# Adding feature tiles on VectorE ahead of the ones-matmuls of two layer norms, in a decoder layer on one core

## The chip, the core and the metric

The kernel runs on one core of a Trainium2 chip. The metric is device time in microseconds (us), the median of several runs. The profile is of one more execution.

## What is computed

One decoder layer on one sequence: x is 256 tokens by 2048 features, in float32. Everything a reader needs here is in the order of the stages and in the layer norm:

```python
mod = silu(c) @ w_ada + b_ada            # shift1, scale1, gate1, shift2, scale2, gate2
u = x*(1+scale1) + shift1
proj = u @ w_in                          # GLU input | q | k | v | two branch gates
hc = silu(layer_norm(causal_conv31(a_lin*sigmoid(a_gate)), conv_ln_g, conv_ln_b))
y_conv = hc @ w_conv_out + b_conv_out    # hc: 256 x 1024
y_attn = causal_attention(rope(q), rope(k), v) @ w_attn_out
mix = (g_conv*y_conv + g_attn*y_attn) @ w_out
x = layer_norm(ALPHA*x + (1+gate1)*mix, ln1_g, ln1_b)
u = x*(1+scale2) + shift2
x = layer_norm(ALPHA*x + (1+gate2)*conv_swiglu(u, w_up, w_down), ln2_g, ln2_b)

def layer_norm(x, g, b):
    mu = x.mean(-1); var = square(x - mu).mean(-1)
    return (x - mu) * rsqrt(var + 1e-5) * g + b
```

## The kernel before

Activations lie feature-major: a tile has 128 features on the partitions and the 256 tokens along the free axis. x is 16 such tiles, in `xT[0]` (0 to 7) and `xT[1]` (8 to 15); the convolution's output `cacc` is 8 tiles.

**Matmuls.** Weights stream through five `raw` buffers of 512 KB (`chunk`, from L380). Each chunk is split into two float32r parts, `wh` (a cast on ScalarE, L393) and `wl` (a subtraction on VectorE, L394), and each product is three matmuls: high by high, high by low, low by high (`feat`, L405 to L407). A `raw` buffer is free again once its `wl` is made.

**adaLN.** The modulation's weights `w_ada` go through the same five buffers, but not to TensorE: VectorE multiplies each chunk by a column of silu(c) and adds it to `acc` (L207). All loads of both kinds are issued by SP, in one queue. So an L207 or L394 that comes late on VectorE holds back the load that wants its buffer, and all loads behind it.

**Background work.** While weights are streamed, `chunk` advances generators: the adaLN pieces, the attention, and a background queue `bg_q` with the convolution, its norm (`conv_norm`, L538) and the first half of the first norm's sums (`ln1_tiles`, L733). Each yields an estimate of its cost; the rates set how much runs per chunk. That gives the program order. The order on each engine is then made by a planner, which simulates the timeline and takes, of the instructions that are ready, the earliest in program order (`schedule_with_timeline_sim=True`).

**The norms.** The mean over features is a sum over partitions and over tiles. It is made on TensorE by a float32 matmul with an all-ones 128 x 128 matrix, one for each tile, accumulated in PSUM; every partition then holds the sum.

- `conv_norm`: 8 ones-matmuls for the mean (L542). Then for each half of four tiles VectorE subtracts the mean (L551, 1024 columns at once), ScalarE squares (L552), and TensorE adds the four squares into `pv` (L554). A small root loads the table (L555). Then the variance (L557), the root (L558), the reciprocal (L560), the products with it (L566), the swish (L568) and the split into `chi` and `clo`, which are the moving operand of the `w_conv_out` matmuls.
- The first norm: `w_out` is streamed in three groups, of tiles 0 to 7, 8 to 11 and 12 to 15. After a group the residual is made (L759). After the first group a rough mean `m0` of two tiles (L764, L765) is subtracted from all tiles, to keep the numbers small: from `xT[1]` in two pieces (L767), from `xT[0]` tile by tile (L735, in `ln1_tiles`, in the background of the second group). `stats` (L725) squares a tile on ScalarE (L728) and adds the tile and its square into the two halves of one PSUM bank, `stat[0]` and `stat[1]` (L729, L730). Tiles 8 to 11 and 12 to 15 get `stats` after their groups. After tiles 8 to 11 the adaLN pieces are run up to the ninth (`ada_until(NB)`), in program order ahead of the third group's weights.
- After the last `stats` the norm is finished (L801 to L807) and the first tiles of `u2h` are made, with which the `w_up` matmuls begin.

Of the kernel before, what the change touches and what calls it, by code (L numbers as in the profile page):

```python
# [8 lines left out]
F32 = mybir.dt.float32  # L9
F32R = mybir.dt.float32r  # L10
AF = mybir.ActivationFunctionType
OP = mybir.AluOpType
# [21 lines left out]
def layer_kernel(ctx: ExitStack, tc: tile.TileContext, x, c, w_ada, b_ada, w_in, conv_dw_w, conv_dw_b,  # L34
# [44 lines left out]

# [1 line left out]
    ident = cst.tile([128, 128], F32, name="ident")  # L81
# [53 lines left out]

# [1 line left out]
    xT = wide(0, F32, "xT")  # L137
# [19 lines left out]

# [1 line left out]
    mod = cst.tile([128, 96], F32, name="mod")  # L159
# [218 lines left out]

# [1 line left out]
    def chunk(src, width, two=False):  # L380
# [61 lines left out]

# [1 line left out]
    lin = slot(6, [128, 8, 256], F32, "lin")  # L444
# [63 lines left out]

# [1 line left out]
    cacc, chi = [None], []  # L510
# [27 lines left out]
    def conv_norm():  # L538
# [10 lines left out]
        for t in range(0, CT, CN):  # L549
            ts = slice(t, t + CN)  # L550
            nc.vector.tensor_tensor(a[:, ts], a[:, ts], mean[:, None, :].to_broadcast([128, CN, 256]), OP.subtract)  # L551
            nc.scalar.activation(sq[:, ts], a[:, ts], AF.Square)  # L552
            for j in range(t, t + CN):
                nc.tensor.matmul(pv[:, :256], ones, sq[:, j], start=j == 0, stop=j == CT - 1)  # L554
        nc.scalar.activation(mean[:, 0:1], sq[:, 7, 0:1], AF.Sqrt)  # L555
# [16 lines left out]

# [1 line left out]
    rps = []  # L574
# [75 lines left out]

# [1 line left out]
    ra0 = 1.0  # L652
# [72 lines left out]
    def stats(t):  # L725
        d = xT[t // 8][:, t % 8]
        sq = wk.tile([128, 256], F32, tag="t", bufs=4, name="sq1")
        nc.scalar.activation(sq, d, AF.Square)  # L728
        nc.tensor.matmul(stat[0], ones, d, start=t == 0, stop=t == KT - 1, skip_group_check=True)  # L729
        nc.tensor.matmul(stat[1], ones, sq, start=False, stop=t == KT - 1, skip_group_check=True)  # L730
        return sq

    def ln1_tiles():  # L733
        for t in range(8):
            nc.vector.tensor_tensor(xT[0][:, t], xT[0][:, t], m0, OP.subtract)  # L735
            stats(t)
            yield 0.34

# [5 lines left out]
    for t0, t1 in zip(cuts, cuts[1:]):  # L744
# [16 lines left out]
        if t0 == 0:  # L761
            pm = pst("pm0")
            for t in range(2):
                nc.tensor.matmul(pm[:, :256], ones, xT[0][:, t], start=t == 0, stop=t == 1)  # L764
            nc.scalar.activation(m0, pm[:, :256], AF.Copy, scale=1.0 / 256)  # L765
            for h in range(2):
                nc.vector.tensor_tensor(xT[1][:, h * 4:h * 4 + 4], xT[1][:, h * 4:h * 4 + 4],  # L767
                                        m0[:, None, :].to_broadcast([128, 4, 256]), OP.subtract)
            pms = pst("pms")
            stat = [pms[:, :256], pms[:, 256:]]  # L770
            bg_q.append(ln1_tiles())
        else:
            for t in range(t0, t1):
                sq = stats(t)
        if t0 == 8:
            nc.scalar.activation(lc[:, 0:1], sq[:, 0:1], AF.Sqrt)
            ada_until(NB)
            drain(bg_q)

# [1 line left out]
    def norm(k, n, center):  # L781
# [38 lines left out]

# [1 line left out]
    NP = 7  # L822
# [49 lines left out]

# [1 line left out]
    lrows = [slot(i, [128, D], F32, n) for i, n in ((14, "l2g"), (15, "l2b"))]  # L874
# [107 lines left out]
```

## Time and profile before

| | |
|---|---|
| median of three runs | 1479.33 us (1477.72 to 1479.35) |
| span of the profiled execution | 1477.4 us |
| TensorE (PE) busy | 1417.7 us, 96% |
| VectorE (DVE) busy | 1108.8 us, 75% |
| ScalarE (ACT) busy | 796.9 us, 54% |
| HBM read | 353.10 MB, 240 GB/s over the span |

In the profile PE is TensorE, DVE VectorE, ACT ScalarE and SP the engine that issues loads. L12 is line 12 of the kernel. A tile's name is followed by its inputs: `wl<-wraw,wh` is `wl` made from `wraw` and `wh`. Times in a timeline count from the start of the span. A busy share of an engine is an average over stages; matmuls are pipelined, and their ends in the trace are modelled. "acc3a" is the fourth PSUM bank of a group, "acc" the adaLN sum.

### The profile page before, as it was taken

The numbers are of one execution on the slowest core, as the hardware profiler recorded it, in microseconds if no ns is written. First come the engines' busy times: TensorE is split into PE (matmuls) and PEld (weight loads), VectorE is DVE, ScalarE is ACT, GpSimd is POOL, SyncE is SP. The second block draws the span as 40 slices with busy tenths as digits, with TensorE's granted clock in tenths as the row PEclk, the third lists the DMA queues.
The fourth block names the chain that finished last, engine by engine and source line by source line (L and its number), as shares of the span: only waits on it lengthen the run. The fifth ranks groups of instructions, "written<-read, shape, count | busy, mean of one in ns | idle before, by whom it ended". The sixth has DMA issues, their size and how long they took to land.

```text
span 1477.4 us, 26835 instructions
## 1 busy us (share of the span) xinstructions
PE 1417.7 (96%) x10691; PEld 1364.2 (92%) x10691; DVE 1108.8 (75%) x1398; ACT 796.9 (54%) x1250; POOL 27.7 (2%) x57
## 2 busy tenths in 40 slices
PE   4899999999999989998999999999999999999996
PEld 4889999989999989997999999999999998888886
DVE  6788888998989879896877767988765545446456
ACT  3546436669987655345545576555444444343342
POOL 2000000210000000000000000000000000000000
PEclk9999999999999999999999999999999999999998
DMA  9999899886567657987799977778776676655662
GB/s 310 328 302 334 299 339 310 256 280 209 175 194 222 210 173 254 310 297 226 242 307 315 323 248 218 240 246 254 238 217 183 180 224 215 193 172 173 189 202 100
DMA packets 154990, 358.53 MB, mean 243 GB/s; under 512 B 12172, under 2 KB 26466, under 8 KB 154608
## 3 DMA queue, kind: packets, MB, share of 16 engines
q1 hardware_dynamic: 152704, 352.37, 74.0%
q0 software_dynamic: 1872, 4.33, 0.9%
q8 instruction: 83, 1.36, 0.4%
q14 instruction: 43, 0.35, 0.1%
q10 hardware_dynamic: 288, 0.12, 0.0%
HBM read 353.10 MB, written 2.10 MB: 240 GB/s over the span
## 4 chain that ended last, share of the span: by engine, by line
PE 75%; DMA 13%; DVE 8%; issue 2%; ACT 2%; SPq 0%; DVEq 0%; ACTq 0%
DMA araw<-in_w_ada_dram 9%; PE acc0a L405 5%; PE acc0a L407 5%; PE acc0a L406 5%; PE acc1a L405 5%; PE acc1a L407 5%; PE acc1a L406 5%; PE acc2a L406 3%; PE acc2a L407 3%; PE acc2a L405 3%; PE acc3a L405 3%; PE acc3a L406 3%; PE acc3a L407 3%; DVE wl L394 3%; DVE acc L207 2%
## 5 line engine op out<-in xcount | busy, mean ns | idle before, releaser
L393 ACT CAST wh<-wraw 128x1024 fp32r<-128x1024 f32 (+1 forms) x483 | 496.7, 1030 | 559.5 <-PE acc3a L416 132.7
L394 DVE TENSOR_TENSOR wl<-wraw,wh 128x1024 fp32r<-128x1024 f32 (+1 forms) x483 | 577.1, 1198 | 252.1 <-ACT wh L393 248.1
L207 DVE SCALAR_TENSOR_TENSOR acc<-araw,ccol,acc 128x1024 f32<-128x1024 f32 (+1 forms) x182 | 225.4, 1238 | 84.3 <-DMA araw<-in_w_ada_dram 82.6
L405 PE MATMUL acc0a<-u2h,wh 128*128 128x256 f32 x352 | 99.3, 282 | 4.8 <-ACT u2h L325 4.8
L407 PE MATMUL acc0a<-u2h,wl 128*128 128x256 f32 x352 | 100.3, 285 | 3.1 <-DVE wl L394 3.1
L405 PE MATMUL acc1a<-u2h,wh 128*128 128x256 f32 x352 | 99.4, 283 | 0.0
L406 PE MATMUL acc0a<-u2l,wh 128*128 128x256 f32 x352 | 99.4, 282 | 0.0
L406 PE MATMUL acc1a<-u2l,wh 128*128 128x256 f32 x352 | 99.2, 282 | 0.0
L407 PE MATMUL acc1a<-u2h,wl 128*128 128x256 f32 x352 | 99.2, 282 | 0.0
L533 ACT ACTIVATE pr<-hc,cw 128x256 f32<-128x256 f32 x200 | 88.8, 500 | 11.7 <-DVE cacc L535 11.3
L405 PE MATMUL acc0a<-uh,wh 128*128 128x256 f32 x256 | 74.9, 292 | 7.1 <-ACT uh L242 7.1
L407 PE MATMUL acc0a<-uh,wl 128*128 128x256 f32 x256 | 74.5, 291 | 3.2 <-DVE wl L394 3.2
L406 PE MATMUL acc0a<-ul,wh 128*128 128x256 f32 x256 | 73.4, 287 | 1.6 <-DVE ul L243 1.6
L405 PE MATMUL acc2a<-uh,wh 128*128 128x256 f32 x256 | 73.1, 286 | 0.5 <-ACT gb L487 0.5
L406 PE MATMUL acc2a<-ul,wh 128*128 128x256 f32 x256 | 73.4, 287 | 0.0
L405 PE MATMUL acc1a<-uh,wh 128*128 128x256 f32 x256 | 73.3, 286 | 0.0
L407 PE MATMUL acc1a<-uh,wl 128*128 128x256 f32 x256 | 73.2, 286 | 0.0
L407 PE MATMUL acc2a<-uh,wl 128*128 128x256 f32 x256 | 73.2, 286 | 0.0
L406 PE MATMUL acc1a<-ul,wh 128*128 128x256 f32 x256 | 73.2, 286 | 0.0
L405 PE MATMUL acc3a<-uh,wh 128*128 128x256 f32 x256 | 73.2, 286 | 0.0
L407 PE MATMUL acc3a<-uh,wl 128*128 128x256 f32 x256 | 73.0, 285 | 0.0
L406 PE MATMUL acc3a<-ul,wh 128*128 128x256 f32 x256 | 72.9, 285 | 0.0
(438 smaller groups left out, 4349.8 us busy)
## 6 DMA issues: line engine op xcount, KB each, us to landing
araw<-in_w_ada_dram SPq DMA_DIRECT2D x176, 512.0 KB, 5.1
wraw<-in_w_up_dram SPq DMA_DIRECT2D x176, 512.0 KB, 4.8
wraw<-in_w_in_dram SPq DMA_DIRECT2D x144, 512.0 KB, 4.9
wraw<-in_w_down_dram SPq DMA_DIRECT2D x55, 512.0 KB, 4.5
wraw<-in_w_down_dram SPq DMA_DIRECT2D x44, 384.0 KB, 3.7
wraw<-in_w_out_dram SPq DMA_DIRECT2D x32, 512.0 KB, 5.5
araw<-in_w_ada_dram SPq DMA_DIRECT2D x32, 256.0 KB, 5.7
wraw<-in_w_attn_out_dram SPq DMA_DIRECT2D x16, 512.0 KB, 4.5
```

Of the source, the lines that this page charges most:

```text
L207: op = nc.vector.scalar_tensor_tensor(acc, r, ccol[:, k:k + 1], acc, OP.mult, OP.add)
L393: nc.scalar.copy(wh, raw)
L394: nc.vector.tensor_tensor(wl, raw, wh.bitcast(F32), OP.subtract)
L405: nc.tensor.matmul(o, wh[:, cs], ah, start=first and i % 2 == 0, stop=False, skip_group_check=True)
L406: nc.tensor.matmul(o, wh[:, cs], al, start=False, stop=False, skip_group_check=True)
L407: nc.tensor.matmul(o, wl[:, cs], ah, start=False, stop=last, skip_group_check=True)
L533: nc.scalar.activation(pr[:, k % 2, i], src, AF.Copy, scale=w)
```

## The change

Tiles are added to each other on VectorE before the ones-matmul, so that fewer ones-matmuls are issued.

- `conv_norm`: the eight squares are added to four and then to two (one instruction of 1024 columns, one of 512), and two ones-matmuls take the place of eight. They now follow both squares.
- `ln1_tiles`: `xT[0]` is centred and squared in two pieces of four tiles. Then the eight tiles, and the eight squares, are each added to four and to two, into `sm`, with two ones-matmuls each. The squares lie in slot 6, the sums in slot 16.
- Tiles 8 to 11 (`ln1_four`): one square of 1024 columns, one add of 512 columns for the tiles and one for the squares, two ones-matmuls each. The background queue is now drained ahead of this, not behind `ada_until(NB)`.
- Tiles 12 to 15 stay as they are.

```diff
@@ conv_norm
             nc.scalar.activation(sq[:, ts], a[:, ts], AF.Square)
-            for j in range(t, t + CN):
-                nc.tensor.matmul(pv[:, :256], ones, sq[:, j], start=j == 0, stop=j == CT - 1)
+        for n in (4, 2):
+            nc.vector.tensor_tensor(sq[:, :n], sq[:, :n], sq[:, n:2 * n], OP.add)
+        for j in range(2):
+            nc.tensor.matmul(pv[:, :256], ones, sq[:, j], start=j == 0, stop=j == 1)
@@ first norm
-        nc.tensor.matmul(stat[0], ones, d, start=t == 0, stop=t == KT - 1, skip_group_check=True)
+        nc.tensor.matmul(stat[0], ones, d, start=False, stop=t == KT - 1, skip_group_check=True)
...
+    def halves(dst, src, n):
+        nc.vector.tensor_tensor(dst[:, :n], src[:, :n], src[:, n:2 * n], OP.add)
+
     def ln1_tiles():
-        for t in range(8):
-            nc.vector.tensor_tensor(xT[0][:, t], xT[0][:, t], m0, OP.subtract)
-            stats(t)
-            yield 0.34
+        sq, sm = slot(6, [128, 8, 256], F32, "sqw"), slot(16, [128, 8, 256], F32, "sm")
+        for h in (slice(0, 4), slice(4, 8)):
+            nc.vector.tensor_tensor(xT[0][:, h], xT[0][:, h], m0[:, None, :].to_broadcast([128, 4, 256]), OP.subtract)
+            nc.scalar.activation(sq[:, h], xT[0][:, h], AF.Square)
+            yield 0.6
+        for j, src in enumerate((xT[0], sq)):
+            s = sm[:, j * 4:j * 4 + 4]
+            halves(s, src, 4)
+            yield 0.5
+            halves(s, s, 2)
+            for i in range(2):
+                nc.tensor.matmul(stat[j], ones, s[:, i], start=j + i == 0, stop=False, skip_group_check=True)
+            yield 0.5
+
+    def ln1_four():
+        sq = slot(6, [128, 8, 256], F32, "sqf")
+        d = xT[1][:, 0:4]
+        nc.scalar.activation(sq[:, 0:4], d, AF.Square)
+        for j, src in enumerate((d, sq[:, 0:4])):
+            s = sq[:, 4 + j * 2:6 + j * 2]
+            halves(s, src, 2)
+            for i in range(2):
+                nc.tensor.matmul(stat[j], ones, s[:, i], start=False, stop=False, skip_group_check=True)
+        return sq[:, 0]
...
+        elif t0 == 8:
+            drain(bg_q)
+            sq = ln1_four()
+            nc.scalar.activation(lc[:, 0:1], sq[:, 0:1], AF.Sqrt)
+            ada_until(NB)
         else:
             for t in range(t0, t1):
-                sq = stats(t)
-        if t0 == 8:
-            nc.scalar.activation(lc[:, 0:1], sq[:, 0:1], AF.Sqrt)
-            ada_until(NB)
-            drain(bg_q)
+                stats(t)
```

## Rows read from the trace of the kernel before

**Rows 1.** The page's first part: busy us, share of the span, instructions.

```profile
PE 1417.7 (96%) x10691; PEld 1364.2 (92%) x10691; DVE 1108.8 (75%) x1398; ACT 796.9 (54%) x1250; POOL 27.7 (2%) x57
```

**Rows 2.** TensorE's waits, 505 to 620 and 620 to 720 us: total, times, longest.

```profile
PE acc0a L405 <- ACT chi L242: 5.3, 1, 5.3
...
PE acc0a L405 <- ACT wh L393: 2.0, 1, 2.0
```

**Rows 3.** Windows: length, busy PE, PEld, DVE, ACT, POOL (instructions), clock, DMA share, GB/s.

```profile
533.20:538.80 5.60, 5.54 (x25) 5.41 (x26) 4.47 (x8) 4.85 (x12) 0.00 (x0) 0.50 0.39 135
...
668.20:671.90 3.70, 3.64 (x18) 3.65 (x19) 2.73 (x4) 2.66 (x7) 0.00 (x0) 0.54 0.85 285
...
540.00:550.00 10.00, 10.00 (x86) 10.00 (x85) 5.75 (x5) 3.14 (x3) 0.00 (x0) 1.00 0.52 156
```

**Rows 4.** VectorE's timeline, 520 to 534 us: start, us, engine, line [idle before].

```profile
520.53 1.22 DVE L394 TENSOR_TENSOR wl<-wraw,wh 128x1024 fp32r<-128x1024 f32 x1
523.57 1.28 DVE L207 SCALAR_TENSOR_TENSOR acc<-araw,ccol,acc 128x1024 f32<-128x1024 f32 x1 [1.82 <-DMA araw<-in_w_ada_dram]
524.77 0.68 DVE L706 TENSOR_TENSOR gb<-acc0a,gb 128x512 f32<-128x512 f32 x1
525.37 1.22 DVE L394 TENSOR_TENSOR wl<-wraw,wh 128x1024 fp32r<-128x1024 f32 x1
...
527.10 0.42 DVE L557 TENSOR_SCALAR pr<-pv 128x256 f32<-128x256 f32 x1
...
530.24 1.22 DVE L394 TENSOR_TENSOR wl<-wraw,wh 128x1024 fp32r<-128x1024 f32 x1
531.36 2.56 DVE L566 TENSOR_TENSOR cacc<-cacc,pr 128x256 f32<-128x256 f32 x5
```

**Rows 5.** VectorE's timeline, 635 to 651 us, columns as in rows 4.

```profile
634.99 2.35 DVE L767 TENSOR_TENSOR xT<-xT,ln 128x1024 f32<-128x1024 f32 x2
637.26 2.10 DVE L735 TENSOR_TENSOR xT<-xT,ln 128x256 f32<-128x256 f32 x6
639.27 1.28 DVE L207 SCALAR_TENSOR_TENSOR acc<-araw,ccol,acc 128x1024 f32<-128x1024 f32 x1
...
641.13 3.49 DVE L394 TENSOR_TENSOR wl<-wraw,wh 128x1024 fp32r<-128x1024 f32 x3
...
649.59 1.28 DVE L207 SCALAR_TENSOR_TENSOR acc<-araw,ccol,acc 128x1024 f32<-128x1024 f32 x1 [2.04 <-DMA araw<-in_w_ada_dram]
```

**Rows 6.** Waits of SP's load queue, 634 to 641 us, columns as in rows 2.

```profile
SPq L190 <- DVE xT L735: 5.4, 1, 5.4
```

**Rows 7.** One window of 2 us, columns as in rows 3.

```profile
640.00:642.00 2.00, 1.48 (x8) 1.19 (x7) 2.00 (x4) 2.00 (x6) 0.00 (x0) 1.00 0.21 25
```

**Rows 8.** The chain that ended last, 637 to 672 us: start, us, what.

```profile
643.52 5.97 DMA araw<-in_w_ada_dram
...
661.84 5.25 DMA wraw<-in_w_out_dram
```

**Rows 9.** VectorE's timeline, 664 to 671 us, columns as in rows 4.

```profile
664.49 3.92 DVE L207 SCALAR_TENSOR_TENSOR acc<-araw,ccol,acc 128x1024 f32<-128x1024 f32 x3
668.32 2.50 DVE L394 TENSOR_TENSOR wl<-wraw,wh 128x1024 fp32r<-128x1024 f32 x2
```

**Rows 10.** The tile `ones`: records, duration ns min/median/max, first and last start.

```profile
L729 PE MATMUL pms<-xT,ones x32: 377/379/484, 639.1 to 696.6; 128*128 128x256 f32 x32
...
L554 PE MATMUL pv<-sq,ones x16: 377/379/379, 523.2 to 526.5; 128*128 128x256 f32 x16
```

**Rows 11.** TensorE's timeline, two successive ones-matmuls, columns as in rows 4.

```profile
642.51 0.59 PE L730 MATMUL pms<-sq,ones 128*128 128x256 f32 x2
642.94 0.59 PE L729 MATMUL pms<-xT,ones 128*128 128x256 f32 x2
```

**Rows 12.** ScalarE's timeline, the squares of the convolution's norm, columns as in rows 4.

```profile
519.67 2.04 ACT L552 ACTIVATE sq<-cacc 128x1024 f32<-128x1024 f32 x2
```

## The prediction

> **What bounds the kernel now.** The page's first part comes first: TensorE is busy for 96% of the span, VectorE for 75% [rows 1]. By that row alone every TensorE microsecond taken out would be a microsecond won. But both changed places stand next to a wait, so the next view is TensorE's waits around them [rows 2]: 5.3 us, ended by ScalarE's `chi` (the convolution branch's output), behind the convolution's norm; and 2.0 us, ended by the cast `wh`, behind the first norm's sums of tiles 8 to 11. After each of the two the windows show a granted clock of 0.50 and 0.54, nearly all at the 1.2 GHz level: 25 matmul records in 5.6 us and 18 in 3.7 us, where a full stretch at 2.4 GHz has 86 in 10 us [rows 3]. A stage that ends in such a wait is set by what ends the wait, not by TensorE's work ahead of it. So I read what ends each.
>
> Wait one (528.0 to 533.3 us). VectorE's timeline [rows 4]: a split ends at 521.75 us, the adaLN step L207 starts at 523.57 us after 1.82 us of waiting for its DMA, and from there VectorE works without a gap up to the `cacc` products at 531.36 us, which feed the swish and `chi`. The variance (L557, 527.10 us) is one link in that row, and two splits that only the next group needs stand in it too (525.37 and 530.24 us). So VectorE's own queue, not only TensorE's sums, makes `chi` late.
>
> Wait two (666.1 to 668.3 us). VectorE's timeline from 635 us [rows 5]: two centrings of 1024 columns, six of the eight one-tile centrings, an adaLN step, the other two, and three splits, back to back; only at 647.5 us does it come to a pause, of 2.04 us, for an adaLN DMA. Each weight buffer is freed by a split or an adaLN step, so that block keeps SP waiting for 5.4 us before it can issue a load [rows 6], and the DMA share falls to 0.21 between 640 and 642 us [rows 7]. From there the chain of waits goes by transfers and VectorE and leaves TensorE out: the adaLN load issued at 643.52 us, then the `w_out` load issued at 661.84 us and landed 5.25 us later, whose cast lets TensorE go on [rows 8]. VectorE is full at the end of it as well: three adaLN steps in a row from 664.49 us and then the first split of the next group, at 668.32 us [rows 9]. So of this stretch VectorE and the loads set the end, and TensorE has time to spare.
>
> **The change part by part.** What it removes: a ones-matmul is two records (16 for 8 matmuls at L554, 32 for 16 at L729, and as many at L730) [rows 10], and two successive ones start 0.43 us apart [rows 11]. The convolution's norm goes from 8 to 2 (6 fewer). The first norm's tiles 0 to 7 go from 16 to 4 (12 fewer), its tiles 8 to 11 from 8 to 4 (4 fewer), tiles 12 to 15 stay. 22 x 0.43 = 9.5 us of TensorE: 2.6 ahead of wait one, 5.2 + 1.7 ahead of wait two.
>
> What it adds is on VectorE. An add of 1024 columns costs what the centring of that size costs: two of them occupy 634.99 to 637.26, 1.14 us each [rows 5]. One of 512 columns costs 0.60 us, the spacing of the L706 at 524.77 us and the split behind it [rows 4]. Convolution's norm: 1.14 + 0.60 = 1.74 us. First norm, tiles 0 to 7: two such pairs, 3.48 us, less what the wide centring saves (eight at 2.01 / 6 = 0.335 us are 2.68; two at 1.14 are 2.28; 0.40 saved) = +3.1 us. Tiles 8 to 11: two adds of 512, +1.2 us. On ScalarE the squares become fewer and wider; it isn't late in either stretch, and I cost that at nothing. No DMA is added. The squares' new slots, 6 and 16, had their last readers in the attention and convolution output stages, so no wait comes from them.
>
> A rule of the Trainium skill speaks the other way. The chain [rows 8] goes through VectorE and loads where TensorE is 96% busy over the span. The Trainium skill, "Perfetto Trace Analysis", section "Identifying the Most-Contended Engine", says to find the engine with the highest occupancy and to optimize that one first (it warns that for TensorE busy time flatters); applied to [rows 1] it makes this change worth the whole 9.5 us, which is the first rival below.
>
> Convolution's norm, on the path. The two adds can start when ScalarE has done the squares, at 521.7 us [rows 12], just when VectorE has its 1.82 us pause [rows 4]. If the planner, which sets each engine's order by its own simulated times, puts them ahead of L207, they are free, and as fewer sums follow, L557 and the products may overtake the two splits in the row, at 1.14 us each (the size of a centring): 2.3 us earlier. If it puts them behind L207, the gapless row gets longer by 1.74 us. Bounds -2.3 and +1.7; neither order is visible in the trace of before, so I take the middle, -0.3. TensorE's 2.6 us are worth nothing of themselves here: it arrives earlier and waits longer.
>
> First norm, tiles 0 to 7. L207 of 639.27 frees the next load's buffer; the two wide centrings stand ahead of it at least (2.28 against 2.01). The adds of the d tiles (1.74 us) are early in program order and ready at once, so they should come before or among the three splits from 641.13 us, and hold the load of 643.52 us back by about 1.74 - 0.40 = 1.3 us. The adds of the squares (1.74 us) come next and fit into the 2.04 us pause before 649.59 [rows 5]. What the load's delay costs is passed on by transfers, which are without a gap from there. Bounds: -0.4 us (all adds in pauses, the centring's saving kept) and +3.1 us (none hidden); taken +1.3.
>
> First norm, tiles 8 to 11. The two adds of 512 want VectorE between the last residuals and the split of 668.32 us, where it has no pause [rows 9]. Bounds 0 (they take a pause that the later loads open) and +1.2; I take +1.2, as the row is full. The 1.7 us saved on TensorE lie in its wait. If that cover were gone they would be a gain of 1.7. A longer wait could also prolong the stretch at 1.2 GHz behind it; the present one costs 3.7 - 18 x 0.116 = 1.6 us [rows 3]. Bound 0 to +1; taken 0, since the clock is down there already.
>
> Sum: -0.3 + 1.3 + 1.2 = +2.2 us. The profiled span is 1477.4 us; the median of the three runs, 1479.33 us, lies 1.9 us above it, and I keep that distance: 1477.4 + 2.2 + 1.9 = 1481.5 us.
>
> **The rivals.** First, TensorE is the limit in spite of the waits: both waits move up with its work, and 9.5 us are won, 1477.4 + 1.9 - 9.5 = 1469.8 us. For it: 96%. Against it: the two waits are ended by other engines, and the removed work lies directly ahead of them.
>
> Second, the convolution's chain gets shorter and VectorE's adds in the first norm disappear in pauses: -2.3 - 0.4 + 0 gives 1476.6 us. For it: the 1.82 us pause at the right moment. Against it: the first norm's adds would have to wait for a pause while they are ready much earlier.
>
> Third, slower: VectorE becomes the bound outright. Its place is the gapless block from 635 us; the adds stand ahead of the steps that free the load buffers, the 5.4 us wait of SP grows by the whole 3.1 us, the adds of tiles 8 to 11 by 1.2 more, and in the convolution's norm they stand behind L207 (+1.7): +6.0, 1485.3 us. It decides from the point where more than the 2.04 us of the pause in adds precede the adaLN step now at 649.59; with one half of it, without the convolution's 1.7, it gives 1483.6.
>
> Fourth, the change doesn't do only what it says: the planner orders all instructions anew, and other stages move by some microseconds in either direction, with the forecast's sum on top.
>
> **How the numbers follow.** About 0.2% (3 us) is what a measurement of this kernel can tell from no change. Forecast 0.45 (it reaches from -1.5 to +3.8 us, about 0.08 of it beyond +3), first rival 0.06, second 0.17 (0.08 of it beyond -3, where TensorE's saved time adds to it), third 0.26, fourth 0.06 (0.02 each way and 0.02 between). Faster 0.06 + 0.08 + 0.02 = 0.16; slower 0.08 + 0.25 + 0.02 = 0.35 (0.01 of the third falls short of +3); same 0.49. The forecast's own range is 1477.8 to 1483.1. Faster and slower cases together hold about half, so the range of 8 in 10 takes in the third rival's sum and most of the second: 1475.0 to 1485.6; the first rival is left out.
>
> **What would show it.** In the profile after: TensorE's records of the sums fall from 80 to 36 (16 + 32 + 32 to 4 + 16 + 16), its busy time by up to 9.5 us less what longer modelled records hide, while the span does not. The wait for `chi` is as long as before or longer, and starts earlier. The wait behind tiles 8 to 11 grows from 2 us to some 9 or 10, and its end moves later by 1 to 4 us against the `chi` wait's end. SP's wait during the centring block is 5.4 us or more. The forecast is wrong if the second wait's end comes closer to the first one's (then TensorE or the freed `wh` buffers did set the loads), or if `chi` moves by more than 2 us, or if a stage that the change doesn't touch moves as much as these.

## The result, and the profile after

| | before | after |
|---|---|---|
| median, runs side by side | 1479.34 us | 1491.31 us |
| ratio | | 1.0076 (95%: 1.0052 to 1.0101) |
| the same pair once more | 1482.54 us | 1491.58 us, 1.0068 (1.0050 to 1.0087) |
| span of the profiled execution | 1477.4 us | 1493.2 us |

The change makes the kernel slower by 0.7 to 0.8%, 9 to 12 us. The prediction (1481.5 us, at most 1485.6) had the sign of its sum right and the size wrong.

Line numbers shift a little: the residual L759 is L784 in after, L706 is L708, the variance L557 is L559, the reciprocal L562, the products L568. The convolution's adds are L554 and its sums L556; the first norm's wide centrings are L741, its adds L736, its sums L750 and L761.

The page's first part of after, against [rows 1]:

```profile
PE 1415.7 (95%) x10647; PEld 1361.0 (91%) x10647; DVE 1115.8 (75%) x1400; ACT 795.7 (53%) x1241; POOL 27.7 (2%) x57
```

The 44 records of the 22 removed ones-matmuls are gone (10691 to 10647), yet TensorE's busy time falls by only 2.0 us and the span grows. So time went into waits. TensorE's waits of after at the two places of [rows 2] (520 to 545 us, 636 to 700 us; total, times, longest):

```profile
PE acc0a L405 <- ACT chi L242: 6.2, 1, 6.2
PE pv L556 <- DVE sq L554: 4.9, 1, 4.9
...
PE acc0a L405 <- ACT wh L393: 6.9, 1, 6.9
PE pms L761 <- DVE sqf L736: 3.5, 1, 3.5
PE acc0a L407 <- DVE wl L394: 2.6, 1, 2.6
```

In before the two waits were 5.3 and 2.0 us. Now two sums wait for adds, and behind each of them the old wait has grown as well. VectorE's timeline of after around the convolution's norm (start, us, engine, line [idle before]), to be held against [rows 4]:

```profile
525.05 1.28 DVE L207 SCALAR_TENSOR_TENSOR acc<-araw,ccol,acc 128x1024 f32<-128x1024 f32 x1 [1.33 <-DMA araw<-in_w_ada_dram]
526.25 1.22 DVE L554 TENSOR_TENSOR sq<-sq 128x1024 f32<-128x1024 f32 x1
527.39 0.68 DVE L708 TENSOR_TENSOR gb<-acc0a,gb 128x512 f32<-128x512 f32 x1
527.99 1.22 DVE L394 TENSOR_TENSOR wl<-wraw,wh 128x1024 fp32r<-128x1024 f32 x1
529.12 0.68 DVE L708 TENSOR_TENSOR gb<-acc1a,gb 128x512 f32<-128x512 f32 x1
529.72 0.68 DVE L708 TENSOR_TENSOR gb<-acc2a,gb 128x512 f32<-128x512 f32 x1
530.32 0.68 DVE L554 TENSOR_TENSOR sq<-sq 128x512 f32<-128x512 f32 x1
...
533.16 0.42 DVE L559 TENSOR_SCALAR pr<-pv 128x256 f32<-128x256 f32 x1 [0.43 <-PE pv L556]
534.07 1.75 DVE L562 RECIPROCAL pr<-pr 128x256 f32<-128x256 f32 x1 [0.48 <-ACT pr L560]
536.21 1.28 DVE L207 SCALAR_TENSOR_TENSOR acc<-araw,ccol,acc 128x1024 f32<-128x1024 f32 x1 [0.38 <-DMA araw<-in_w_ada_dram]
537.41 2.56 DVE L568 TENSOR_TENSOR cacc<-cacc,pr 128x256 f32<-128x256 f32 x5
```

The first add stands behind the adaLN step. The second, which needs the first, stands behind a split and three L708. An adaLN step has also come between the reciprocal and the products. TensorE's timeline in the same stretch:

```profile
525.89 0.28 PE L407 MATMUL acc3a<-ohi,wl 128*128 128x256 f32 x1
531.05 2.07 PE L556 MATMUL pv<-sq,ones 128*128 128x256 f32 x4 [4.88 <-DVE sq L554]
...
539.30 0.58 PE L405 MATMUL acc0a<-chi,wh 128*128 128x256 f32 x1 [6.17 <-ACT chi L242]
```

It had finished its products at 526 us, earlier than before, and stood for 4.88 us. The four records that then came took 2.07 us; before, twice as many took 1.89 us. From the end of the split ahead of the norm to the first `chi` product it is 15.6 us (523.72 to 539.30), before 11.5 us (521.75 to 533.26).

The first norm: the queue of loads (start, us, lines, tile, count; the time is from the first issue to the last), of after and, below it, of before:

```profile
654.27 18.41 SPq L190 DMA_DIRECT2D araw<-in_w_ada_dram  x10
673.63 12.29 SPq L384 DMA_DIRECT2D wraw<-in_w_out_dram  x8
```

```profile
645.85 15.03 SPq L190 DMA_DIRECT2D araw<-in_w_ada_dram  x10
661.84 11.52 SPq L384 DMA_DIRECT2D wraw<-in_w_out_dram  x8
```

Ten adaLN loads stand ahead of the third group's weights, and each needs a buffer that VectorE frees. They take 18.4 us in place of 15.0, and the third group's first weights are asked for 11.8 us later on the clock of the trace (7.7 us of that are there already at 626 us, ahead of this stage). The two windows behind it (columns as in [rows 3]):

```profile
671.00:681.00 10.00, 3.09 (x9) 2.15 (x8) 6.59 (x7) 1.33 (x3) 0.00 (x0) 0.67 0.83 268
681.00:688.00 7.00, 6.96 (x35) 6.67 (x36) 4.53 (x4) 3.09 (x4) 0.00 (x0) 0.56 0.75 235
```

TensorE works 3.1 us of ten, and the next 7 us run mostly at the 1.2 GHz level: 35 records, where 7 us at 2.4 GHz hold 60 (86 in 10 us, [rows 3]).

**Where the time went, by stage.** Each of these kernels makes the same 483 weight casts (L393) in the same order. The difference in the start of the same cast, against the profiled run of before, tells where time is lost. Conv: between the casts that before has at 506.4 and 571.4 us. Between: 571.4 to 626.2. Norm: 626.2 to 693.9. Up: 693.9 to 900.8 us. Beside it the length of the ten adaLN loads and TensorE's longest wait for `wh` behind them (all in us; kernels explained below):

```
kernel                    ratio    conv  between  norm   up    ten loads  wh wait
before, second trace        -      -0.6   -0.1    -0.5  -2.2     15.0       2.1
after                     1.0076   +4.0   +2.1    +6.3  +1.8     18.4       6.9
after, second trace       1.0068   +4.7   +1.5    +5.1  +1.9     18.5       6.4
e1 conv part              1.0077   +4.4   +0.8    +0.4  +4.9     15.5       1.0
e2 norm part              1.0022    0.0   -0.8    +4.2  +1.8     17.0       7.5
e3 fewer sums, no adds    1.0059   +2.0   +1.6    +5.0  +3.8     19.1       8.0
e4 all sums, and adds     1.0035   +2.0   +1.0    +2.4  +3.0     17.0       4.8
e5 = e3, order of before  1.0019   +0.6   -0.7    +1.3  +2.5     14.7       3.8
e6 = e1, order of before  0.9997    0.0   -0.2    +0.1  -0.3     15.0       2.0
e7 = after, order of bef. 1.0030   +0.8   +0.6    +3.3  +0.8     16.5       5.6
e8 = before, order of e3  1.0066   +2.1   +1.1    +9.0  +2.7     21.5       7.4
e9 = e8's norm part       1.0031   -0.9   +0.4    +5.1  +1.9     19.0       8.0
e10 = e8's conv part      1.0018   +1.5   +0.5    +1.3  +2.5     15.9       2.0
e11 = e7, sums later      1.0032   +0.6   +1.2    +1.9  +5.7     16.9       7.8
e12 = before, conv chain  1.0028   +1.6   +1.0     0.0  +2.2     15.0       2.4
e13 = e7, conv chain      1.0042   +0.3   +1.4    +2.0  +2.8     16.1       5.2
```

Nearly three quarters of the loss of after lie in the two changed stages, in both traces: 10.3 of 14.2 us, 9.8 of 13.2 (the trace of before is one of its shorter runs, so these totals are larger than the medians' difference). The column "up" differs by 2.2 us between two traces of before alone, so nothing of that size is read from it. The other columns move too where nothing in their stage was changed: conv by 0.0 and -0.9 us (e2, e9), norm by -0.5 to +1.3 us (before's second trace, e1, e6, e10). A single figure of about 1 us in them shows nothing by itself.

### The profile page after: what moved, and what is told of

The parts are those of the page before. It is cut to its first block, busy times and chain, and to the rows that moved or that the text cites. A ratio compares the mean times of both kernels' runs of the same rounds, so it can differ in the third digit from the quotient of the medians.

```text
span 1493.2 us, 26737 instructions
## 1 busy us (share of the span) xinstructions
PE 1415.7 (95%) x10647; PEld 1361.0 (91%) x10647; DVE 1115.8 (75%) x1400; ACT 795.7 (53%) x1241; POOL 27.7 (2%) x57
## 4 chain that ended last, share of the span: by engine, by line
PE 75%; DMA 12%; DVE 8%; issue 3%; ACT 2%; SPq 0%; DVEq 0%; ACTq 0%
DMA araw<-in_w_ada_dram 9%; PE acc0a L407 5%; PE acc0a L405 5%; PE acc0a L406 5%; PE acc1a L407 5%; PE acc1a L405 5%; PE acc1a L406 5%; PE acc2a L406 3%; PE acc2a L407 3%; PE acc2a L405 3%; PE acc3a L405 3%; PE acc3a L407 3%; PE acc3a L406 3%; DVE wl L394 3%; DMA wraw<-in_w_in_dram 2%
## 5 line engine op out<-in xcount | busy, mean ns | idle before, releaser
L393 ACT CAST wh<-wraw 128x1024 fp32r<-128x1024 f32 (+1 forms) x483 | 496.5, 1029 | 571.2 <-PE acc3a L416 132.9
L394 DVE TENSOR_TENSOR wl<-wraw,wh 128x1024 fp32r<-128x1024 f32 (+1 forms) x483 | 577.3, 1199 | 258.5 <-ACT wh L393 255.5
L207 DVE SCALAR_TENSOR_TENSOR acc<-araw,ccol,acc 128x1024 f32<-128x1024 f32 (+1 forms) x182 | 225.5, 1239 | 79.4 <-DMA araw<-in_w_ada_dram 78.2
L405 PE MATMUL acc0a<-u2h,wh 128*128 128x256 f32 x352 | 99.7, 283 | 5.7 <-ACT u2h L325 4.8
L405 PE MATMUL acc1a<-u2h,wh 128*128 128x256 f32 x352 | 99.6, 283 | 0.0
L405 PE MATMUL acc0a<-uh,wh 128*128 128x256 f32 x256 | 74.8, 292 | 7.4 <-ACT uh L242 7.4
L405 PE MATMUL acc2a<-uh,wh 128*128 128x256 f32 x256 | 73.1, 286 | 0.5 <-ACT gb L487 0.5
L405 PE MATMUL acc1a<-uh,wh 128*128 128x256 f32 x256 | 73.4, 287 | 0.0
L405 PE MATMUL acc3a<-uh,wh 128*128 128x256 f32 x256 | 73.1, 286 | 0.0
L405 PEld LDWEIGHTS acc0a<-u2h,wh 128*128 128x128 f32 x352 | 67.1, 191 | 6.3 <-ACT u2h L325 5.2
```

Source lines behind the costliest of these rows:

```text
L207: op = nc.vector.scalar_tensor_tensor(acc, r, ccol[:, k:k + 1], acc, OP.mult, OP.add)
L393: nc.scalar.copy(wh, raw)
L394: nc.vector.tensor_tensor(wl, raw, wh.bitcast(F32), OP.subtract)
L405: nc.tensor.matmul(o, wh[:, cs], ah, start=first and i % 2 == 0, stop=False, skip_group_check=True)
```

## The experiments

**First, the change in parts.** Theory and rivals of these four: sums that wait for adds in VectorE's queue (Q), VectorE's added time (V), TensorE as the limit (T).

`e1_conv_only`: only the hunk in `conv_norm`.

> The change in the convolution's norm alone (two VectorE adds, two sums instead of eight); the first norm is that of before. Theory Q, queues: the sums wait for adds that stand between other VectorE work, and everything behind them in the two engines' queues waits too. Then this part alone costs what the trace of after shows between the mean of the norm and chi, 6.0 less the 1.6 us that were there already: +4.4 us, 1483.7 us, with TensorE's wait for the adds near 4.9 us. Theory V, VectorE's time: only the 1.74 us of adds count, +1.7 us or less, 1481.1. Theory T, TensorE is the bound: -2.6 us.

Measured: 1.0077 (1.0053 to 1.0101), the wait for the second add 5.0 us, `chi` 6.3 us, the stage +4.4 us. This part alone brings the stage's whole loss, as Q had it. But its time is 11 us over before's, far more than Q's 4.4: another 4.9 us lie in the up-projection. There the planner gave this kernel a new order as well: six adaLN steps and a split stand at other places in VectorE's queue, and one cast in ScalarE's. What that order costs wasn't measured apart.

`e2_norm1_only`: only the hunks of the first norm.

> The change in the first norm alone (tiles 0 to 11); the convolution's norm is that of before. Theory Q: the wait for the adds of tiles 8 to 11 (3.5 us) and the longer wait for the third group's first cast (6.9 instead of 2.0 us) come back without the convolution's part: +5 to +7 us, 1484.3 to 1486.3 us. Theory V: 3.1 + 1.2 = +4.3 us at most, without the wait for the adds. Theory T: -6.9 us. If the two parts added up to much less than the 12 us of the whole, a third cause is open.

Measured: 1.0022 (1.0006 to 1.0038), the stage +4.2 us, `wh` 7.5 us and the sums of tiles 8 to 11 3.5 us. In time this is +3.3 us, under Q's 5 to 7 and within V's 4.3; the waits are those that Q named.

`e3_fewer_sums_no_adds`: the 22 sums left out, nothing put in their place.

```diff
-            for j in range(t, t + CN):
-                nc.tensor.matmul(pv[:, :256], ones, sq[:, j], start=j == 0, stop=j == CT - 1)
+            j = 0 if t == 0 else CT - 1
+            nc.tensor.matmul(pv[:, :256], ones, sq[:, j], start=j == 0, stop=j == CT - 1)
...
+        if t in (0, 7, 8, 11) or t > 11:
...
```

> The kernel before with 22 of its 40 ones-matmuls left out and no add on VectorE in their place, so the norms are made from part of the tiles. It is the worth of TensorE's 9.5 us by itself. Theory T: -9.5 us, 1469.8 us. Theories Q and V: the waits for chi and for the third group's weights swallow it, -3 to 0 us, 1476.3 to 1479.3 us.

Measured: 1.0059 (1.0035 to 1.0082). T falls: with 9.5 us less for TensorE and nothing more for anyone, the kernel is slower, nearly as much as after. Q and V don't explain it either, as there are no adds. This run changed the question: something that comes with fewer sums, not with adds, makes most of the loss.

`e4_adds_only`: all 40 sums, and the adds made into spare tiles that nobody reads.

```diff
+        gh = slot(11, [128, 8, 256], F32, "gh")
+        nc.vector.tensor_tensor(gh[:, :4], sq[:, :4], sq[:, 4:], OP.add)
+        nc.vector.tensor_tensor(gh[:, :2], gh[:, :2], gh[:, 2:4], OP.add)
...
+            nc.vector.tensor_tensor(s, xT[0][:, 0:4], xT[0][:, 4:8], OP.add)
+            nc.vector.tensor_tensor(s[:, 0:2], s[:, 0:2], s[:, 2:4], OP.add)
...
```

> The kernel before with VectorE adds of the same sizes and number put in at the same places, into tiles that nothing reads; all 40 ones-matmuls stay. It is the cost of VectorE's 6.4 us of adds by itself, with nobody waiting for them. Theory V: +4 to +6 us, 1483.3 to 1485.3 us. Theory Q: most of the loss is in the waiting for the adds, so this costs less, 0 to +3 us.

Measured: 1.0035 (1.0021 to 1.0049), +2.0 us and +2.4 us in the two stages. Around the convolution's norm the rest of VectorE's row stands as in before, with the two adds put in behind the adaLN step; so the 2.0 us are what the prediction's +1.7 bound had priced, adds in a gapless row. V holds as a part. In the first norm the planner moved splits and adaLN steps too, so the 2.4 us there are not the adds' alone.

**Second, order against work.** The planner sets each queue's order from its own simulated times; other times give another order, for instructions that the change doesn't touch too. The new theory (P) is that this order is the loss; the rival (W) that the work itself is. These kernels fix the order of the three queues with a chain of ordering edges (that the edges cost time themselves is unlikely: e6 has them and runs as fast as before):

```python
for a, b in zip(places, places[1:]):
    order(seq[a], seq[b])
```

Lines stand 15 further down in them: L420 is L405, L409 is L394, L222 is L207, L399 is L384.

`e8_all_sums_new_order`: the kernel before, all its work, in the order that the planner gave e3. Of VectorE's 1398 places 27 differ, of ScalarE's 1178, 16. VectorE's queue behind tiles 0 to 7 of the first norm, before and then (`acc` is an adaLN step, `xT1` a residual of tiles 8 to 11):

```
before: acc wl acc acc acc wl acc acc acc xT1 xT1 acc xT1 xT1 acc acc acc
e8:     wl acc wl acc acc acc xT1 xT1 acc xT1 xT1 acc acc acc acc acc acc
```

> The kernel before with all its 40 ones-matmuls and no adds, its queues held in the order that the planner made for e3 (the left out sums next to those that e3 keeps). Its work is that of before; only the order is new. Theory P: most of e3's loss comes back, +4 to +10 us. Theory W: no difference, -1 to +1 us.

Measured: 1.0066 (1.0046 to 1.0086). The same instructions in another order cost nearly as much as the change. Its loads:

```profile
650.01 21.52 SPq L205 DMA_DIRECT2D araw<-in_w_ada_dram  x10
672.48 11.79 SPq L399 DMA_DIRECT2D wraw<-in_w_out_dram  x8
```

`e5_fewer_sums_old_order`: e3's work in before's order.

> The kernel of e3 (22 ones-matmuls left out, nothing added, so the norms are made from part of the tiles), with the instructions of VectorE, ScalarE and TensorE held in the order in which they stand in the kernel before. Against e3 only that order differs: 27 places of 1398 on VectorE, 16 of 1178 on ScalarE, and TensorE's. Theory P, the planner's order: e3's loss of 0.6% goes, and TensorE's saved time can show: 0 to -5 us against the kernel before. Theory W, the work itself: it stays at e3's +8 us. Theory T of e3 in full, TensorE is the bound: -9.5 us.

Measured: 1.0019 (1.0006 to 1.0032), down from 1.0059. TensorE's waits in it, at the two places:

```profile
PE acc0a L420 <- ACT chi L257: 8.3, 1, 8.3
...
PE acc0a L420 <- ACT wh L408: 3.8, 1, 3.8
```

They have grown by 3.0 us (2.6 us of sums went) and by 1.8 us; TensorE arrives earlier and waits longer. The order is what e3 lost most by, but the time is not in P's range of 0 to -5 us. Why it is even slower than before, by 0.2%, stays open: 2.5 us of it lie in the up-projection, which I don't read.

`e6_conv_placed`: the convolution's part, with before's order and both adds together right behind the squares, ahead of the adaLN step.

> The change in the convolution's norm alone, as e1, but with all queues held in the order of the kernel before, the two adds placed one behind the other right behind the first split after the centring, ahead of the adaLN step, and the two sums where the last of the eight stood. Theory P: e1's loss goes; the adds lie in VectorE's 1.8 us pause and chi is not later, 0 to -3 us against before. Theory W: the adds delay chi wherever they stand, +2 to +4.4 us, as e1 in that stage.

Measured: 0.9997 (0.9983 to 1.0011), the stage 0.0 us. VectorE's timeline:

```profile
525.17 1.95 DVE L569 TENSOR_TENSOR sq<-sq 128x1024 f32<-128x1024 f32 x2
527.04 1.28 DVE L222 SCALAR_TENSOR_TENSOR acc<-araw,ccol,acc 128x1024 f32<-128x1024 f32 x1
```

The pause of 1.82 us ahead of this step [rows 4] is gone, the adds lie in it. They are free there. The sums of TensorE are worth nothing here; `chi`'s wait grows to 7.3 us.

`e7_all_placed`: the whole change in before's order, the convolution's part as in e6, the first norm's adds of tiles 0 to 7 where the pause of 2.04 us was [rows 5], those of tiles 8 to 11 behind the third group's first two splits.

> The whole change, with the queues held in the order of the kernel before: the convolution's adds as in e6, the first norm's adds of tiles 0 to 7 in VectorE's pause behind the second adaLN step after the centring, their four sums where the last of the sixteen stood, the adds of tiles 8 to 11 behind the second split of the third group and their four sums just ahead of those of tile 12, where nobody waits for them. Against the changed kernel only the order differs. Theory P: most of the 12 us goes, -4 to +2 us against before. Theory W: +6 to +12 us stay.

Measured: 1.0030 (1.0015 to 1.0044), against 1.0076 with the planner's order. The conv stage is back within 0.8 us; the first norm keeps +3.3 us. TensorE's waits there:

```profile
PE pms L765 <- DVE sm L751: 5.6, 1, 5.6
PE acc0a L420 <- ACT wh L408: 5.6, 1, 5.6
```

Against before it is +4.4 us, between P's range (up to +2) and W's (from +6). P holds for the larger part, 0.46 of 0.76%; W for what is left in the first norm.

**Third, which places of the order.** `e9_norm_vector_order`: before, with only the VectorE row of e8 shown above.

> The kernel before with nothing added or left out, and with sixteen places of VectorE's queue changed, as the planner set them when sums were left out: behind tiles 0 to 7 of the first norm the splits of two w_out chunks and the residuals of tiles 8 to 11 go ahead of adaLN steps that stood before them. ScalarE and TensorE keep the order of before. Theory L (loads: VectorE waits at the residuals for TensorE, the adaLN steps behind them free their row buffers later, and the third group's w_out loads, which follow ten adaLN loads in SyncE's queue, start later): the ten adaLN loads take 17 to 20 us in place of 15.0, the first w_out load of the third group is issued 2 to 5 us later, TensorE's wait for wh there grows from 2.0 to 5 to 7 us, and the time is 3 to 6 us over before's, ratio 1.002 to 1.004. Rival N (the loss in this stage was TensorE's own new order and ScalarE's, not VectorE's): the ten loads take 15 to 16 us and the ratio is 0.999 to 1.001.

Measured: 1.0031 (1.0014 to 1.0048), the stage +5.1 us. L holds, at the upper end of its numbers (the wait for `wh` is 8.0 us, over its 5 to 7), and N falls: the ten loads take 19.0 us. VectorE and the loads:

```profile
661.39 0.88 DVE L774 SCALAR_TENSOR_TENSOR xT<-acc0a,g,xT 128x256 f32<-128x256 f32 x2 [1.28 <-PE acc0a L422]
...
664.16 7.88 DVE L222 SCALAR_TENSOR_TENSOR acc<-araw,ccol,acc 128x1024 f32<-128x1024 f32 x6
674.08 2.55 DVE L409 TENSOR_TENSOR wl<-wraw,wh 128x1024 fp32r<-128x1024 f32 x2 [2.03 <-ACT wh L408]
```

```profile
646.83 19.01 SPq L205 DMA_DIRECT2D araw<-in_w_ada_dram  x10
666.79 12.37 SPq L399 DMA_DIRECT2D wraw<-in_w_out_dram  x8
```

Six adaLN steps are left behind the residuals in place of three [rows 9]. Splits that went ahead of them wait for their casts (2.75 and 1.67 us at 651 and 655 us), the residual waits for TensorE, and the adaLN steps wait behind them. With them wait the buffers, the loads and the third group's weights.

`e10_conv_vector_order`: before, with only the conv part of e8's order.

```
before: L557 L706 L560 L706 wl L566 clo acc clo
e10:    L706 L557 L706 wl L560 L566 acc clo clo
```

> The kernel before with nothing added or left out, and with seven places of VectorE's queue and two of ScalarE's changed around the convolution's norm: the variance (L557) goes behind two L706 and the reciprocal (L560) behind two L706 and a split of weights, and one cast of weights goes ahead of the square root. Theory P (the norm's chain is what TensorE waits for, and each VectorE instruction put into it lengthens it): 0.6 us each for the L706 and 1.2 us for the split put the end of the chain 1.5 to 2.5 us later, chi's wait grows from 5.3 to 6.5 to 8, and the time is 1 to 3 us over before's, ratio 1.0007 to 1.002. Rival N: the chain has that room, chi's wait stays at 5 to 5.8 and the ratio is 0.9995 to 1.0005.

Measured: 1.0018 (1.0003 to 1.0032), the stage +1.5 us. TensorE's waits:

```profile
PE acc0a L420 <- ACT chi L257: 5.8, 1, 5.8
...
PE acc0a L421 <- DVE clo L258: 1.0, 1, 1.0
```

The time is as P said, but its account is not: `chi`'s wait grew by 0.5 us, not by 1.2 or more, since the same instructions as in before stand ahead of the products, only in another sequence. The larger part, 1.0 us, is a new wait for `clo`, and this order puts an adaLN step ahead of the first `clo`, a swap that the expectation doesn't name. 0.31% and 0.18% are most of e8's 0.66%; the rest (TensorE's and ScalarE's own order, four places later in VectorE's queue) wasn't taken apart.

`e11_all_placed_late`: e7, with the four sums of tiles 0 to 7 moved on TensorE to where it waits for the third group.

> The whole change with the queues held to the order of before as in the earlier placed version, and one thing moved: the four sums of tiles 0 to 7 stand on TensorE just ahead of the third group's first product, where TensorE waits for weights anyway, and no longer ahead of the second group's last products. Theory L (the third group starts when its w_out loads are in, and these follow the adaLN steps on VectorE, which the adds delay): TensorE's wait of 5.6 us for the sums goes, its wait for wh stays at 4 to 8 us, the first w_out load of the third group comes at most 2 us earlier, and the ratio goes from 1.003 to 1.001 to 1.0025. Theory T (TensorE's own waits are the time): the 5.6 us come back whole, ratio 0.999 to 0.9995.

Measured: 1.0032 (1.0018 to 1.0046); nothing gained. The wait of 5.6 us for the sums is gone, and the wait for `wh` went from 5.6 to 7.8 us, that for `wl` from 2.4 to 4.7:

```profile
PE acc0a L420 <- ACT wh L408: 7.8, 1, 7.8
PE acc0a L422 <- DVE wl L409: 4.7, 3, 2.1
```

T falls again. The norm's stage is 1.4 us shorter than e7's, as L has it, but the ratio is over L's numbers: this trace lost 5.7 us in the up-projection, in a queue order that is e7's (+0.8 there). I have no cause for that.

`c0_before_again`: the kernel before, a second trace.

> The kernel before once more, for a second trace of the same program: it tells how far stretches that the change leaves alone move from run to run. If the up-projection from 700 to 880 us (DMA busy 0.92) varies by itself, the gaps between its weight casts differ by 2 to 5 us from the first trace in that stretch; if it repeats within 1 us, then the 2 to 6 us by which the changed kernels were longer there come from their order or their work.

Measured: 1479.64 us. It was 3.9 us behind the first trace at 250 us, still 2.7 us at 694 us, and only 0.5 us at 901 us. So the up-projection does vary by itself, by 2.2 us here.

**Fourth, the other direction.** If a longer chain through VectorE costs time, a shorter one might gain it. `e12_before_short_chain`: before, the two splits of [rows 4] that only the next group needs moved behind the products.

```
before: L706 wl L706 L557 L706 L560 L706 wl L566 clo acc clo
e12:    L706 L706 L557 L706 L560 L706 L566 clo wl clo wl acc
```

> The kernel before with nothing added or left out; two splits of weights that only the next group needs leave VectorE's chain from the variance to the products of the convolution's norm (they stood at 525.4 and 530.2 us, ahead of L557 and of L566) and go behind the products, ahead of the adaLN step. Theory P (what stands in VectorE's chain makes chi late, and TensorE only waits for it): chi comes 2.3 us earlier, its wait falls from 5.3 to about 3 us, and the ratio is 0.998 to 0.9995, if the later loads give nothing back. Rival G (given back: the two buffers come free 1 to 6 us later, and with them the loads of the next group): chi's wait falls as much, a wait for wh or wl of 1 to 3 us comes in the next group, and the ratio is 0.9995 to 1.0005.

Measured: 1.0028 (1.0013 to 1.0044): slower, outside both. `chi`'s wait fell by 1.3 us, to 4.0. But the loads and VectorE:

```profile
525.63 12.88 SPq L403 DMA_DIRECT2D wraw<-in_w_conv_out_dram  x3
539.66 0.33 SPq L207 DMA_DIRECT2D araw<-in_w_ada_dram  x1
```

```profile
543.86 1.28 DVE L222 SCALAR_TENSOR_TENSOR acc<-araw,ccol,acc 128x1024 f32<-128x1024 f32 x1 [4.26 <-DMA araw<-in_w_ada_dram]
545.07 1.89 DVE L258 TENSOR_TENSOR clo<-cacc,chi 128x512 fp32r<-128x512 f32 x3
```

The three loads take 12.9 us; in before they took 5.2:

```profile
521.78 5.17 SPq L388 DMA_DIRECT2D wraw<-in_w_conv_out_dram  x3
```

The adaLN load comes late, VectorE waits 4.26 us for it, and three `clo` that TensorE needs stand behind. Between the casts of 506.4 and 588.8 us this kernel loses 4.7 us, of which 2.0 come back by 626.2 us. Moving the splits gives back more than it gains: they free load buffers.

Why `chi` gained only 1.3 of the 2.3 us shows in the variance, which now stands idle for the sums:

```profile
530.94 0.42 DVE L572 TENSOR_SCALAR pr<-pv 128x256 f32<-128x256 f32 x1 [1.23 <-PE pv L569]
```

With the two splits out of the chain, TensorE's eight sums are its next link.

`e13_all_short_chain`: e7 with the same.

> The whole change with the queues held to the order of before as in the first placed version, and the same two splits behind the products of the convolution's norm. Theory P: the ratio is that of the first placed version, 1.003, less what the short chain brought the kernel before, so 1.001 to 1.0025; above 1.003 if nothing is gained. If TensorE's saved work became worth something once VectorE's chain is shorter, the ratio would fall below 1.0005.

Measured: 1.0042 (1.0028 to 1.0056), with e7 at 1.0030: nothing gained here either. With two sums in place of eight the variance doesn't wait for them, and moving the splits shortens `chi`'s wait by 2.8 us (from e7's 7.9 to 5.1), in e12 by 1.3. So once the splits are out, fewer sums do help the chain. But the loads give it back as in e12: the three take 11.8 us, and VectorE waits 4.09 us for the adaLN load.

`c1_after_again`: after, a second trace and three more rounds.

> The changed kernel once more, for a second trace and more timed runs. If the two stages of the change carry the loss, the trace has again 3 to 5 us lost between the weight casts on both sides of the convolution's norm and 5 to 8 us around the first norm, the waits of 4 to 5 us for the second add and of 6 to 8 us for wh, and what the up-projection adds may differ by 3 us from the first trace. Ratio 1.005 to 1.01.

Measured: 1.0068, and the same five waits within 0.5 us. The stages' losses repeat, +4.7 and +5.1 us.

No kernel here beats the one before. The best of them, e6, has only the convolution's part and cannot be told from it.

## Why the prediction was right or wrong

**What it removes and what an add costs: right.** The sums go from 80 records to 36, and 9.5 us of TensorE's work are worth nothing. The adds take what they were priced at: in after the two of the convolution's norm hold VectorE for 1.14 and 0.59 us. The first rival is out: in e5 the work is gone and the order kept, and no time comes back. The rule of the Trainium skill that was weighed ("Perfetto Trace Analysis", section "Identifying the Most-Contended Engine") points at the engine that is 96% busy; e5, e6 and e11 show that here its time was not the one to save. (The Trainium skill's warning there is that TensorE's matmul busy share is not a good measure, with the busy share of the weight loads as one to take instead; that is 92% in [rows 1] and points at the same engine.)

**The convolution's norm: wrong, +4.0 and +4.7 us outside the bounds of -2.3 to +1.7.** The step that failed is the upper bound, which priced two adds that stand together behind the adaLN step (1.74 us). The trace of before had shown already that VectorE's row has no pause behind that step, and the second add depends on the first. The planner put a split and three L708 between the two and an adaLN step between reciprocal and products. From the end of the adaLN step to the variance it was 2.3 us, it is 6.8, where two adds alone would have made 4.0. The lower bound was false too: e12 shows that the two splits can't be overtaken without loss. The case "ahead of L207, they are free" was right (e6), but the planner didn't choose it.

**The first norm: the sum comes near what a fixed order gives, and the order was not fixed.** 1.3 + 1.2 = 2.5 us were predicted. With the order held, e7 and e11 lost 3.3 and 1.9 us in this stage, with adds at other places than those that were priced; so this tests the sum and not each term. The planner's order gives 6.3 and 5.1. The step that failed here is that the sum took every instruction that the change doesn't name as staying where it stood. e9 moves only such instructions, adds none, and loses 5.1 us. The two are not simply added: in after's own order the adds stand among the adaLN steps.

**The path named for it was right, the place on it wrong.** AdaLN steps on VectorE free buffers, these let the loads go, and the third group waits for them: in the table the losses of the norm's stage rise, on the whole, with the length of the ten loads, from 0 us at 15.0 to 9.0 us at 21.5. Ahead of these ten loads SP's waits for buffers that an L207 frees went from 5.6 us in six to 10.5 us in six. But the load that the adds of tiles 0 to 7 were to hold back by 1.3 us, that of 643.52 us, isn't late. Counted from the first wide centring (L767, in after L792) it is issued at 8.5 us in before and at 8.1 us in after; the adds came behind it, among the splits and adaLN steps. The delay comes with the ten loads: the third group's first is issued at 26.9 us in before and at 31.0 us in after.

**The rivals.** The third, VectorE as the bound, is the nearest in place, but its 6.0 us come from adds in the queue, and that is the smaller part. The fourth, a new order of all instructions, was the main one. It got 0.06 and no price, "by some microseconds in either direction". The new order could not be read from the trace of before, but a price for it could have been estimated there: behind their pauses the two places have no slack on VectorE [rows 4, 5, 9], so an instruction that is put ahead can cost up to its length (0.6 to 1.3 us). Taking two out gave nothing back (e12). A slip in the third rival: 1483.6 is its sum without the convolution's 1.7 and with the whole 3.1 us, not with a half.

**What would show it.** The wait behind tiles 8 to 11 was to grow to 9 to 10 us: it is 3.5 + 6.9 = 10.4, right. Its end against the end of `chi`'s wait was to move by 1 to 4 us: before 668.26 - 533.26 = 135.0, after 680.86 - 539.30 = 141.6, so 6.6, wrong. The wait for `chi` was to be as long or longer and to start earlier: it is longer (6.2 us), but starts later (at 533.1 us, before 528.0), as TensorE waits for the second add first. SP's wait in the centring block was to be 5.4 us or more, and is 4.2: ahead of the adaLN step that ends it stands one wide centring where six narrow ones stood (1.13 us against 2.01), and not both, as the working had it. TensorE's busy time fell by 2.0 us, within "up to 9.5". Of the signs named against the forecast, the move of `chi` by over 2 us came true.

**Left open.** The up-projection's part: after +1.8 and +1.9 us in two traces, e1 +4.9, e11 +5.7, with two traces of before 2.2 us apart. I don't know how much of it belongs to the order: after, e1, e3 and e8 have a new order in VectorE's queue there too, e7 and e11 have that of before. Nor was the work of before run in after's own order (e8 has e3's); for after, the weight of the order rests on e7. So of the 13 to 14 us between the traces about 10 are explained by the two stages, and 3 to 4 by nothing shown.

## What to carry to other kernels

Where a planner orders in-order queues from simulated times, an edit is two changes: its own work, and a new order for its neighbours. Measure them apart by holding the old order, and price the new order where a queue has no pause. Work taken off an engine ahead of a wait may only make the wait longer (e5: 2.6 us of sums went, the wait grew by 3.0); ask first what ends that wait, and which buffers the instructions in that chain give back.

## What the runs showed that I had not expected

- 27 of VectorE's 1398 places and 16 of ScalarE's 1178, with TensorE's order to match and the same work, are worth 0.66% (e8). Sixteen of VectorE's places alone are worth 0.31% (e9).
- An instruction that looks like filler in a chain can carry the loads. Two splits moved by a few us turned 5.2 us of three loads into 12.9 us (e12).
- After 4.88 us of waiting, TensorE made two ones-matmuls in 2.07 us (granted clock 0.50 between 530 and 540 us). Before, at 1.00, four took 1.89 us. So here the wait that was put ahead of the sums made the sums slower as well.
